# Bias lines of a four-layer attention kernel: 24 copies written from many partitions, and the later layers' lines made in the first layer

## The chip, the cores and the metric

One NeuronCore of a Trainium2 chip runs the whole program in one launch. The metric is device time in microseconds (us), the median of the runs. The engines are named as the profile names them: PE (TensorE, matrix products), PEld (its weight loads), DVE (VectorE), ACT (ScalarE), POOL (GpSimd) and SP, the engine that issues all DMAs of this kernel on one queue.

## The reference

The input is 512 tokens of 1,024 channels. Four layers follow one another, each `x + mixer(rms_norm(x) @ w_in) @ w_out`, in float32:

```
A  sliding-window attention (window 128, 16 heads of 64, 4 key heads),
   logits + head_bias(rel_table, query - key), a sink per head, SiLU gate
B  sparse attention in three branches over one shared key/value side:
   compressed keys (31 blocks of 32 tokens through a small MLP),
   selected blocks (all of at most 8), window (512, the whole sequence);
   each with head_bias(rel_table, distance)
C  twice: mLSTM (4 heads), gated linear attention (2 x 2 heads), and
   attention over the 128 best keys of a cheap index score,
   logits + rel_bias[t5_bucket(key - query)] (4 heads of 128)
```

`head_bias` is a table lookup: 32 buckets of distance (exact up to 16 or 8, logarithmic above) by heads. The bias of a pair of tokens depends on their distance alone, so the bias matrix of a head is constant along its diagonals.

## The kernel before

The tokens are 4 blocks of 128 on the partitions. `norm_x` normalizes x and transposes it into a high and a low half (`xhi`, `xlo`). Every projection is three products a step (`gemm_n_slices`, L262 to L264, and `gemm_t_slices`, L282 to L284). Weights come in pieces: `load` fills one of three buffers `wraw` by a DMA on SP (L228), `split` makes the halves `whi` (ACT, L235) and `wlo` (DVE L237, POOL L247) in one of five. Which weights follow which is written out as a plan; the loads of the next projection are spread over the present one. Attention runs as steps (queries, scores, values, done), and projections are woven between the steps by hand-written lists (`FILL_A`, `FILL_B`, `EVENTS`).

The order of the instructions on each engine's queue is not that of the program text: a scheduler at build time plays the program through with a cost model and puts each engine's instructions, the DMA issues on SP too, into the order in which they would become ready. On the chip each queue then runs strictly in that order. Tiles with a tag share a fixed number of buffers: the tag `E` has 4 (`epage`). It holds the exponentials of the attention, the split weights of the compression MLP, and the small pages of the bias code.

The bias code. `table33` puts a table of 32 buckets with a row of -1e30 below it into SBUF as [33, heads]. `toeplitz` multiplies it with a constant one-hot matrix [33, 384] (L369), which gives a line: the bias at distances 255 to -128 for each head. The result is copied out of PSUM (L371) and written to DRAM 128 times over (L373), from as many partitions as there are heads. `toeplitz_read` then reads a matrix [128 queries, heads, 256 keys] in which each query starts one element earlier than the one before it (L378); each query reads a copy of its own:

```
d = s.dram.tile([P, nh, 384], F32, name=name)
nc.sync.dma_start(d.rearrange("q h u -> h q u"), sb[:, None, :].to_broadcast([nh, P, 384]))
```

There are three lines. line_a (16 heads) is made in layer A behind the keys, line_b (16 heads) at the start of layer B, line_d (4 heads) in `consts_c` at the start of the first layer C. Each group of four heads of A and B reads its `bias` when its queries are projected; each of the two tasks of two heads in each layer C reads `dbias` (L1617). Layer B makes besides a bias `cb` for its compressed keys: four loads of one-hot pages (L816), 16 products (L817), one copy (L818).

Of the kernel before, what the change touches and what calls it, by code (L numbers as in the profile page):

```python
# [21 lines left out]
NT = 4  # L22
# [54 lines left out]
class Ctx:  # L77
# [25 lines left out]
    def banks(s, name, t, sc):  # L103
        """8 banks: products of the projections, transposes, scores, values"""
        s.PSB = {"g": 2, "t": t, "s": sc, "o": 1}
        s.ps = s.pool(name, 1, space=PSUM)
# [28 lines left out]
    def rstd(s, ss, n, width, tag, bufs=2):  # L135
        """1 / sqrt(ss / width + EPS): first guess from the exponent, Newton"""
# [15 lines left out]
    def bcast_row(s, pool, src, n, name, **kw):  # L152
        """[n] in DRAM -> [P, n]"""
        t = pool.tile([P, n], F32, name=name, **kw)
        s.nc.sync.dma_start(t, bass.AP(tensor=src.tensor, offset=src.offset, ap=[[0, P], [1, n]]))
        return t

# [1 line left out]
    RAW, HI = 3, 5  # L159

    def w(s, key):
        """the weights of this name; those that follow in the plan are loaded and split in the course of their use"""
# [16 lines left out]
    def prefetch(s, held, blocks):  # L179
        """queues the next loads of the plan: [(part of the present use behind it, what to emit)]; held: pieces in use, free one by one in the last block"""  # L180
# [20 lines left out]
    def progress(s, n):  # L201
        """n products of the present use are emitted"""
# [11 lines left out]
    def piece(s, out, segs, kt0, u, n, ku, width, gain=None):  # L214
        """segs: list of (dram 2d AP, column, width, column in tile). out: (hi, lo, width) per kt"""
# [37 lines left out]
    def gemm_n_slices(s, wts, width, evac, lhs=None, toks=range(NT), tag="g"):  # L253
        """out[tok, width] = x @ w, three passes; stops after every 12 products"""
# [20 lines left out]
    def gemm_t_slices(s, wts, cols, evac, tag="g"):  # L275
        """out[cols, tok] = (x @ w)^T for each range of 128 columns."""
# [15 lines left out]
    def x_rstd(s, t):  # L292
        """1 / rms of block t of x"""
# [19 lines left out]
    def norm_x(s, gain=None):  # L313
        """x / rms(x) * gain -> xhi, xlo; without a gain the weights bring it"""
# [21 lines left out]
    def load_gains(s):  # L336
        """the gains of the two norms of the second layer: those of 128 channels in a column"""
# [9 lines left out]
    def to_T(s, o, oT, ts):  # L347
        """o [P, 256] -> oT (hi, lo) [P, 2, ts]"""
# [14 lines left out]
    def toeplitz(s, table33, nh, line, name):  # L363
        """[33, nh] table and [33, 384] one-hot line -> DRAM [P, nh, 384], P times the same; [h, u]: the bias at distance 255 - u"""
        nc = s.nc
        ln = s.epage()[:33, :384]
        nc.sync.dma_start(ln, s.ia[line])
        ps = s.bk("t")
        nc.tensor.matmul(ps[:nh, :384], table33, ln, start=True, stop=True)  # L369
        sb = s.epage()[:nh, :384]  # L370
        nc.vector.tensor_copy(sb, ps[:nh, :384])  # L371
        d = s.dram.tile([P, nh, 384], F32, name=name)
        nc.sync.dma_start(d.rearrange("q h u -> h q u"), sb[:, None, :].to_broadcast([nh, P, 384]))  # L373
        return d

    def toeplitz_read(s, out, d, h0, nh):
        """out [P, nh, 256]: query p, key column k' of the blocks (previous, own): distance p + 128 - k'"""
        s.nc.sync.dma_start(out, bass.AP(tensor=d.tensor, offset=d.offset + h0 * 384 + 127,  # L378
                                         ap=[[d.shape[1] * 384 - 1, P], [384, nh], [1, 256]]))

    def table33(s, src, nh, name):
        t = s.cst.tile([33, nh], F32, name=name)
        s.nc.sync.dma_start(t[:32], src)
        s.nc.vector.memset(t[32:33], NEG)
        return t

# [1 line left out]
    def silu2(s, out, ps, th=None):  # L388
        """2 * silu(ps)"""
# [6 lines left out]
    def sumsq(s, out, src, sq, nh, hd, eng=None):  # L396
        """src [P, nh * hd] in SBUF -> out [P, nh] sums of squares"""
# [8 lines left out]
    def q_group(s, wts, wk, out):  # L406
        """projects 4 query heads and their gates; -> (raw queries [P, NT, 256], 1 / rms [P, NT * 4]), [2 * silu(gate)] per block"""
# [15 lines left out]
    def q_packs(s, q, t, wk):  # L423
        """queries of 4 heads, block t: normalized, -> [(hi 64, lo 64), head, tok] in F32R"""
# [13 lines left out]
    def q_packs2(s, q, t, wk):  # L438
        """queries of 4 heads, block t: normalized, -> for each pair of heads [(hi; hi) / (lo; lo), tok] in F32R"""
# [19 lines left out]
    def k_pack(s, kv, out, wk, bank="t", tag="qs"):  # L459
        """keys [P, heads, 64] -> out [(hi; lo), heads, tok] in F32R"""  # L460
# [10 lines left out]
    def half(s):  # L471
        """the next half of the bank o"""
# [10 lines left out]
    def pipeline_slices(s, steps):  # L483
        """attention steps, each in its stages behind those of its followers; yields the part of a step's work behind it"""
# [9 lines left out]
    def weave(s, main, fill):  # L494
        """main yields the part of the whole that is behind it; fill: [(number, products)], spread over it"""
# [14 lines left out]
    def pipeline(s, steps, fill):  # L510
        """attention steps, each in its stages behind those of its followers; fill: products [(first step, last step, number, slices)], one after the other"""
# [22 lines left out]
    def k_packs(s, kr, r, gain, kT, wk, t):  # L534
        """kr [P, 256] raw keys of 4 heads, r [P, 4]; kT[:, h, 0 / 1, tok]: (hi; hi) / (lo; lo)"""
# [16 lines left out]
    def out_plan(s, src, kt0):  # L552
        """the loads of 256 rows of src"""
        return [([(src, n * 512, 512, 0)], kt0, 2, 512) for n in range(2)]

    def w_out_slices(s, ws, lhs):
        """x += y[:, rows] @ the weights of these rows"""
# [20 lines left out]
# projections spread over the steps of the attention: from, to  # L578
# [3 lines left out]
def layer_a(s):  # L582
    nc, tc, ia = s.nc, s.tc, s.ia
    outer = s.stack
    with ExitStack() as st:
# [6 lines left out]
        # per-head constants  # L592
# [8 lines left out]
        # keys and values  # L601
# [19 lines left out]
        def project(g):  # L621
            """queries and gates of four heads"""
# [8 lines left out]
        class Step:  # L631
            """block t of the queries of group g"""
# [68 lines left out]
        for _ in project(0):  # L701
            pass
        what = {"q": (96, project), "o": (48, out)}
# [9 lines left out]
def compress(s, wk, R, w1, w2, posT):  # L713
    """R 2 x [P (head, chunk), 8 * 64] -> 2 * silu(flat @ w1), transposed: [P hidden, 2, P rows], and w2 [P, 2, 64]"""
# [57 lines left out]
# projections spread over the steps of the attention: from, to  # L772
# [4 lines left out]
def layer_b(s):  # L777
    nc, tc, ia = s.nc, s.tc, s.ia
    outer = s.stack
    with ExitStack() as st:  # L780
# [8 lines left out]
        # gains  # L789
# [9 lines left out]
        cb = lp.tile([P, 16, 16], F32, name="cb")  # L799
        gt = lp.tile([P, NT, 48], F32, name="gt")  # L800

        line = s.toeplitz(s.rel33, 16, "c_line_b", "line_b")
        # position embeddings: [(l 2, d), kt] by a transpose
# [7 lines left out]
        # bias of the compressed keys: [query, head, chunk - 8 * block + 8]  # L811
        pt = s.bk("t")
        for c in range(16):
            if c % 4 == 0:
                oc = s.epage()[:33].rearrange("p (a b) -> p a b", a=4)
                nc.sync.dma_start(oc, ia["c_cmp"][:, c:c + 4])  # L816
            nc.tensor.matmul(pt[:, c * 16:(c + 1) * 16], oc[:, c % 4], s.rel33, start=True, stop=True)  # L817
        nc.vector.tensor_copy(cb, pt[:, :256].rearrange("p (c h) -> p h c", h=16))  # L818
        # compressed branch: raw keys and values bounce to (head, chunk) rows
# [8 lines left out]
        # selected and window branches  # L828
        def rescale(t):
            """the gain of the queries' norm comes on to block t"""  # L830
# [41 lines left out]
        # keys of the compressed branch  # L872
# [11 lines left out]
        # values of the compressed branch, block diagonal over the heads of a group  # L884
# [869 lines left out]
```

## Time and profile before

| what | value |
|---|---|
| median of 3 runs | 2139.19 us (2138.87 to 2147.04) |
| span of the profiled execution, first to last instruction | 2134.7 us (no own time is listed beside it) |
| busy: PE, PEld, DVE, ACT, POOL | 1995.8, 1647.8, 1402.0, 928.7, 920.5 us |
| DMA | 168.58 MB, 79 GB/s in the mean |

A row of a timeline gives the start, the time, the engine, the line of the kernel, the operation with what it writes and reads, the number of instructions that are merged into the row, and in brackets the idle time of the engine ahead of it with what ended that. SPq is SP's DMA queue. Products of the PE overlap, so the distance of their starts counts, not their duration.

### The profile page before, as it was taken

What the parts mean: (1) busy time and instruction counts of PE and PEld (TensorE: products, weight loads), DVE (VectorE), ACT (ScalarE), POOL (GpSimd) and SP (SyncE); (2) the same over time, 40 slices, a digit from 0 to 9 for tenths busy, and PEclk for the clock granted to TensorE, in tenths of its full rate; (3) what the DMA queues carried; (4) which work ended last, traced back from release to release, by engine and by line L of the source; (5) the groups of instructions that cost most, each with busy time, mean ns of one, the idle gap of its engine ahead of it and who ended that gap; (6) DMA issues with size and microseconds to landing.
All of it is one profiled execution on the core that took longest, in us unless ns stands there. A gap on an engine that the chain in (4) does not pass through costs nothing.

```text
span 2134.7 us, 30245 instructions
## 1 busy us (share of the span) xinstructions
PE 1995.8 (93%) x10211; PEld 1647.8 (77%) x10211; DVE 1402.0 (66%) x3717; ACT 928.7 (44%) x2153; POOL 920.5 (43%) x866
## 2 busy tenths in 40 slices
PE   7789969999999998599899999999999999999999
PEld 6678857788888887377778788887777778788887
DVE  6267736846555576279986965556579976965555
ACT  4355425555454554254442433434454432433433
POOL 3434413544544431133765453344234755453343
PEclk9989989999999999799999999999999999999999
DMA  5632265321221101322222223232222222223231
GB/s 171 94 98 67 75 90 143 114 79 50 71 64 47 60 8 45 79 77 69 67 82 87 80 76 95 68 102 76 80 79 66 77 76 83 80 76 101 62 103 44
DMA packets 161339, 168.58 MB, mean 79 GB/s; under 512 B 25797, under 2 KB 135964, under 8 KB 161184
## 3 DMA queue, kind: packets, MB, share of 16 engines
q1 hardware_dynamic: 161184, 166.65, 27.5%
q8 instruction: 81, 1.33, 0.3%
q14 instruction: 74, 0.61, 0.1%
HBM read 155.08 MB, written 11.53 MB: 78 GB/s over the span
## 4 chain that ended last, share of the span: by engine, by line
PE 55%; DVE 15%; issue 4%; DMA 3%; POOL 1%; ACT 1%; SPq 0%; DVEq 0%; POOLq 0%; ACTq 0%
PE b_g L262 10%; PE b_g L263 10%; PE b_g L264 10%; PE b_g L282 3%; PE b_g L283 3%; PE b_g L284 3%; PE b_o L1059 2%; DVE wlo L237 2%; DVE topw L1310 2%; DMA line_d<-E 2%; PE b_s L1029 2%; DVE m L1309 1%; PE b_t L1052 1%; PE b_o L1536 1%; DMA wraw<-in_w_in_dram 1%
## 5 line engine op out<-in xcount | busy, mean ns | idle before, releaser
L247 POOL TENSOR_TENSOR wlo<-wraw,whi 128x512 fp32r<-128x512 f32 (+1 forms) x314 | 462.7, 1493 | 370.4 <-ACT whi L235 338.0
L262 PE MATMUL b_g<-whi,xhi 128*128 128x512 f32 x1280 | 508.2, 398 | 10.8 <-DVE my L1493 5.6
L264 PE MATMUL b_g<-whi,xlo 128*128 128x512 f32 x1280 | 508.2, 397 | 2.0 <-DVE xlo L360 2.0
L263 PE MATMUL b_g<-wlo,xhi 128*128 128x512 f32 x1280 | 507.3, 397 | 0.0
L235 ACT ACTIVATE whi<-wraw 128x1024 fp32r<-128x1024 f32 (+2 forms) x250 | 260.8, 1045 | 194.1 <-PE b_g L264 87.1
L262 PEld LDWEIGHTS b_g<-whi,xhi 128*128 128x128 f32 x1280 | 242.7, 190 | 64.2 <-issue 6.0
L264 PEld LDWEIGHTS b_g<-whi,xlo 128*128 128x128 f32 x1280 | 242.8, 190 | 54.1 <-DVE xlo L360 3.4
L263 PEld LDWEIGHTS b_g<-wlo,xhi 128*128 128x128 f32 x1280 | 242.7, 190 | 47.8 <-POOL wlo L247 0.4
L237 DVE TENSOR_TENSOR wlo<-wraw,whi 128x512 fp32r<-128x512 f32 (+2 forms) x198 | 188.4, 955 | 104.2 <-ACT whi L235 101.3
L282 PE MATMUL b_g<-xhi,whi 128*128 128x512 f32 x400 | 162.7, 407 | 29.5 <-ACT whi L235 22.8
L562 DVE TENSOR_TENSOR x<-x,b_g 128x512 f32<-128x512 f32 x192 | 130.1, 680 | 55.2 <-PE b_g L264 53.9
L283 PE MATMUL b_g<-xlo,whi 128*128 128x512 f32 x400 | 159.9, 400 | 0.0
L284 PE MATMUL b_g<-xhi,wlo 128*128 128x512 f32 x400 | 159.6, 399 | 0.2 <-POOL wlo L247 0.2
L282 PEld LDWEIGHTS b_g<-xhi,whi 128*128 128x128 f32 x400 | 75.9, 190 | 51.5 <-ACT whi L235 24.0
L284 PEld LDWEIGHTS b_g<-xhi,wlo 128*128 128x128 f32 x400 | 75.8, 189 | 19.0 <-issue 1.5
L283 PEld LDWEIGHTS b_g<-xlo,whi 128*128 128x128 f32 x400 | 75.9, 190 | 17.8 <-issue 2.5
L1059 PEld LDWEIGHTS b_o<-v,PT 128*128 128x128 f32 x640 | 82.1, 192 | 8.1 <-DVE PT L1055 3.2
L1493 DVE SCALAR_TENSOR_TENSOR my<-b_g,vec,my 128x511 f32<-128x511 f32 (+2 forms) x96 | 71.5, 744 | 21.3 <-ACT my L1490 19.9
L1059 PE MATMUL b_o<-v,PT 128*128 128x64 f32 x640 | 82.3, 269 | 3.3 <-DVE PT L1055 2.8
L957 POOL TENSOR_TENSOR og<-og,sz 128x256 f32<-128x256 f32 x32 | 24.3, 760 | 140.5 <-DVE og L951 132.4
L1499 POOL TENSOR_TENSOR mT<-my,mT 128x512 fp32r<-128x512 f32 x32 | 45.8, 1438 | 86.8 <-ACT mT L1498 52.8
L1039 ACT ACTIVATE E<-E,nm 128x256 f32<-128x256 f32 (+1 forms) x128 | 60.8, 476 | 35.2 <-DVE nm L1038 35.2
(419 smaller groups left out, 4150.7 us busy)
## 6 DMA issues: line engine op xcount, KB each, us to landing
wraw<-in_w_in_dram SPq DMA_DIRECT2D x240, 256.0 KB, 3.1
wraw<-in_b_w_in_dram SPq DMA_DIRECT2D x64, 256.0 KB, 3.1
wraw<-in_w_out_dram SPq DMA_DIRECT2D x32, 512.0 KB, 3.6
wraw<-in_w_in_dram SPq DMA_DIRECT2D x24, 512.0 KB, 4.8
wraw<-in_a_w_in_dram SPq DMA_DIRECT2D x32, 256.0 KB, 2.8
wraw<-in_kv_w_dram SPq DMA_DIRECT2D x12, 512.0 KB, 3.9
wraw<-in_a_w_out_dram SPq DMA_DIRECT2D x8, 512.0 KB, 3.5
wraw<-in_b_w_out_dram SPq DMA_DIRECT2D x8, 512.0 KB, 3.8
```

Source lines behind the costliest of these rows:

```text
L235: nc.scalar.activation(hi[:, :n, c], raw[:, :n, c], AF.Copy)
L237: nc.vector.tensor_tensor(lo[:, :h, c], raw[:, :h, c], hi[:, :h, c].bitcast(F32), OP.subtract)
L247: nc.gpsimd.tensor_tensor(lo[:, js, c], raw[:, js, c], hi[:, js, c].bitcast(F32), OP.subtract)
L262: nc.tensor.matmul(ps[:, :width], xh, h[:, :width], start=k == 0, stop=False)
L263: nc.tensor.matmul(ps[:, :width], xh, l[:, :width], start=False, stop=False)
L264: nc.tensor.matmul(ps[:, :width], xl, h[:, :width], start=False, stop=k == n - 1)
L282: nc.tensor.matmul(ps, h[:, c * P:(c + 1) * P], s.xhi[:, k], start=k == 0, stop=False)
L283: nc.tensor.matmul(ps, h[:, c * P:(c + 1) * P], s.xlo[:, k], start=False, stop=False)
L284: nc.tensor.matmul(ps, l[:, c * P:(c + 1) * P], s.xhi[:, k], start=False, stop=k == n - 1)
L562: nc.vector.tensor_tensor(s.x[:, t, n * 512:(n + 1) * 512], s.x[:, t, n * 512:(n + 1) * 512], ps, OP.add)
L1059: nc.tensor.matmul(bl.po[:, h * 64:(h + 1) * 64], PT[:, k * P:(k + 1) * P], v[b][:, k, g * 64:(g + 1) * 64], start=k == 0, stop=k == t)
L1493: nc.vector.scalar_tensor_tensor(y[:, j:], ps[:, :SEQ - j], w, y[:, j:], op0=OP.mult, op1=OP.add)
```

## The change

A line is written in 24 copies instead of 128. For that the table is repeated along its columns (8 times for 16 heads, 24 times for 4), so that one product gives a line for each copy and head on a partition of its own; three products, copies and writes make the 24 copies of a line of 16 heads, one of each those of a line of 4 heads. Query p = 16 a + b of a read uses copy a + b. A read is split into one DMA for each head. The lines of B and C and the bias `cb` are made in layer A, right behind the projection of its first four query heads; `cb` and the wider tables lie in the pool of constants. Comments and docstrings go too.

```
+    COPIES = 24
     def toeplitz(s, table33, nh, line, name):
         nc = s.nc
         ln = s.epage()[:33, :384]
         nc.sync.dma_start(ln, s.ia[line])
-        ps = s.bk("t")
-        nc.tensor.matmul(ps[:nh, :384], table33, ln, start=True, stop=True)
-        sb = s.epage()[:nh, :384]
-        nc.vector.tensor_copy(sb, ps[:nh, :384])
-        d = s.dram.tile([P, nh, 384], F32, name=name)
-        nc.sync.dma_start(d.rearrange("q h u -> h q u"), sb[:, None, :].to_broadcast([nh, P, 384]))
+        d = s.dram.tile([s.COPIES, nh, 384], F32, name=name)
+        n = min(s.COPIES, P // nh)
+        for c in range(0, s.COPIES, n):
+            ps = s.bk("t")
+            nc.tensor.matmul(ps[:n * nh, :384], table33[:, :n * nh], ln, start=True, stop=True)
+            sb = s.epage()[:n * nh, :384]
+            nc.vector.tensor_copy(sb, ps[:n * nh, :384])
+            nc.sync.dma_start(d[c:c + n].rearrange("q h u -> (q h) u"), sb)
         return d
     def toeplitz_read(s, out, d, h0, nh):
-        s.nc.sync.dma_start(out, bass.AP(tensor=d.tensor, offset=d.offset + h0 * 384 + 127,
-                                         ap=[[d.shape[1] * 384 - 1, P], [384, nh], [1, 256]]))
+        w = d.shape[1] * 384
+        for h in range(nh):
+            s.nc.sync.dma_start(out[:, h], bass.AP(tensor=d.tensor, offset=d.offset + (h0 + h) * 384 + 127,
+                                                   ap=[[w - 16, 8], [w - 1, 16], [1, 256]]))
     def table33(s, src, nh, name):
-        t = s.cst.tile([33, nh], F32, name=name)
-        s.nc.sync.dma_start(t[:32], src)
-        s.nc.vector.memset(t[32:33], NEG)
+        nc, n = s.nc, min(s.COPIES, P // nh)
+        t = s.cst.tile([33, n * nh], F32, name=name)
+        nc.sync.dma_start(t[:32, :nh], src)
+        nc.vector.memset(t[32:33], NEG)
+        nc.vector.tensor_copy(t[:32, nh:].rearrange("p (n h) -> p n h", h=nh), t[:32, None, :nh].to_broadcast([32, n - 1, nh]))
         return t
+    def later_biases(s):
+        nc = s.nc
+        s.line_b = s.toeplitz(s.rel33, 16, "c_line_b", "line_b")
+        s.line_d = s.toeplitz(s.table33(s.ia["rel_bias_2"], 4, "rel33d"), 4, "c_line_d", "line_d")
+        s.cb = s.cst.tile([P, 16, 16], F32, name="cb")
+        pt = s.bk("t")
+        for c in range(0, 16, 4):
+            oc = s.epage()[:33].rearrange("p (a b) -> p a b", a=4)
+            nc.sync.dma_start(oc, s.ia["c_cmp"][:, c:c + 4])
+            for j in range(4):
+                nc.tensor.matmul(pt[:, (c + j) * 16:(c + j + 1) * 16], oc[:, j], s.rel33[:, :16], start=True, stop=True)
+        nc.vector.tensor_copy(s.cb, pt[:, :256].rearrange("p (c h) -> p h c", h=16))
...
# layer_a
         for _ in project(0):
             pass
+        s.later_biases()
...
# layer_b
-        cb = lp.tile([P, 16, 16], F32, name="cb")
+        cb, line = s.cb, s.line_b
-        line = s.toeplitz(s.rel33, 16, "c_line_b", "line_b")
-        pt = s.bk("t")
-        for c in range(16):
-            if c % 4 == 0:
-                oc = s.epage()[:33].rearrange("p (a b) -> p a b", a=4)
-                nc.sync.dma_start(oc, ia["c_cmp"][:, c:c + 4])
-            nc.tensor.matmul(pt[:, c * 16:(c + 1) * 16], oc[:, c % 4], s.rel33, start=True, stop=True)
-        nc.vector.tensor_copy(cb, pt[:, :256].rearrange("p (c h) -> p h c", h=16))
...
# consts_c
-    t = s.table33(ia["rel_bias_2"], 4, "rel33d")
-    s.line_d = s.toeplitz(t, 4, "c_line_d", "line_d")
```

## Rows read from the trace of the kernel before

**Rows 1.** The page: the span, and PE busy in tenths of 40 slices.

```profile
span 2134.7 us, 30245 instructions
PE   7789969999999998599899999999999999999999
```

**Rows 2.** Busy time by stretch: PE, PEld, DVE, ACT, POOL, granted clock, DMA share, GB/s.

```profile
94.70:114.80 20.10, 0.03 (x2) 0.06 (x1) 0.68 (x7) 0.00 (x0) 1.70 (x2) 0.58 0.81 125
114.80:120.00 5.20, 5.20 (x21) 4.55 (x22) 3.26 (x19) 3.30 (x13) 2.04 (x3) 0.65 0.94 308
303.90:322.90 19.00, 0.43 (x2) 0.01 (x1) 0.00 (x0) 0.13 (x1) 0.00 (x0) 0.65 0.88 111
322.90:332.00 9.10, 9.05 (x33) 7.91 (x34) 3.98 (x6) 3.17 (x8) 2.38 (x2) 0.60 0.88 273
867.20:890.10 22.90, 0.16 (x1) 0.00 (x0) 0.00 (x1) 1.06 (x1) 0.00 (x0) 0.55 0.26 42
...
120.00:260.00 140.00, 139.99 (x886) 123.80 (x885) 104.46 (x341) 69.91 (x219) 63.13 (x66) 1.00 0.22 70
980.00:1100.00 120.00, 108.93 (x515) 87.72 (x513) 118.05 (x264) 53.25 (x94) 76.57 (x74) 1.00 0.27 82
```

**Rows 3.** Timeline of SP and DVE in layer A.

```profile
76.43 0.35 SPq L373 DMA_DIRECT2D line_a<-E  x1
110.22 0.92 SPq L378 DMA_DIRECT2D bias<-line_a  x2
...
75.86 0.53 DVE L371 COPY E<-b_t 16x384 f32<-16x384 f32 x1
...
114.12 0.29 DVE L660 CUSTOM_DVE_ANT_0 E<-b_s,bias 128x128 f32<-128x128 f32 x1 [26.90 <-DMA bias<-line_a]
```

**Rows 4.** Timeline of PE in layer A.

```profile
88.45 0.67 PE L657 MATMUL b_s<-kT,qT 128*128 128x128 f32 x5
...
94.09 0.39 PE L264 MATMUL b_g<-whi,xlo 128*128 128x512 f32 x1
94.32 0.39 PE L262 MATMUL b_g<-whi,xhi 128*128 128x512 f32 x1
114.78 2.05 PE L657 MATMUL b_s<-kT,qT 128*128 128x256 f32 x8 [20.07 <-DVE mx L660]
```

**Rows 5.** Timelines of SP and PE in layer B.

```profile
288.11 0.33 SPq L373 DMA_DIRECT2D line_b<-E  x1
...
293.76 1.95 PE L817 MATMUL b_t<-rel,E 33*128 33x16 f32 x16
...
322.95 3.60 PE L817 MATMUL b_t<-rel,E 33*128 33x16 f32 x16 [18.62 <-DMA E<-in_c_cmp_dram]
```

**Rows 6.** Timelines of SP, PE, ACT and POOL in layer C.

```profile
854.04 0.27 SPq L373 DMA_DIRECT2D line_d<-E  x1
...
887.62 0.39 SPq L378 DMA_DIRECT2D dbias<-line_d  x1
...
890.12 0.80 PE L282 MATMUL b_g<-xhi,whi 128*128 128x512 f32 x1 [22.76 <-ACT whi L235]
...
897.67 0.50 PE L282 MATMUL b_g<-xhi,whi 128*128 128x512 f32 x1 [2.17 <-DVE ik L360]
...
889.01 1.06 ACT L235 ACTIVATE whi<-wraw 128x1024 fp32r<-128x1024 f32 x1 [29.29 <-DMA wraw<-in_w_in_dram]
...
857.49 3.50 POOL L247 TENSOR_TENSOR wlo<-wraw,whi 128x512 fp32r<-128x512 f32 x2 [0.81 <-ACT whi L235]
```

**Rows 7.** A stretch of line_a's write; DMA issues: KB each, us to landing.

```profile
76.40:88.00 11.60, 11.60 (x54) 9.28 (x53) 1.84 (x5) 4.42 (x10) 2.71 (x4) 1.00 0.79 90
...
kvd<-kvc SPq DMA_DIRECT2D x4, 256.0 KB, 2.2
dbias<-line_d SPq DMA_DIRECT2D x4, 256.0 KB, 3.5
```

**Rows 8.** Timeline of PE: the line product of layer A.

```profile
74.95 0.82 PE L369 MATMUL b_t<-E,rel 33*16 33x384 f32 x2
```

## The prediction

> **What bounds the kernel now.** I read the page first. TensorE (PE) is busy nearly everywhere; only a few of the forty slices (of 53.4 us) stand at 5 to 8 tenths after the start, and slices 2, 3, 6, 17 lie where bias lines are written [rows 1]. Then I cut those places into stretches at the ends of the PE's waits [rows 2]: in 94.7 to 114.8, 303.9 to 322.9 and 867.2 to 890.1 us all five engines together do almost nothing (PE 0.03, 0.43 and 0.16 us). These are no shifts of load between engines; everything stops. The reader should see in the same rows that the clock granted to the PE is 0.55 to 0.65 there, that is, it has gone to the lower level (1.2 GHz) after an idle PE, and is still low in the two stretches that follow here; and that from 120 to 260 the PE has no gap at all, so what is lost in a stop is not won back behind it.
>
> The timelines name each stop. In the first layer (A) one write of line_a goes out at 76.43, the reads of bias and the weight loads behind them leave SP only at 110.22, and VectorE (DVE) waits 26.90 us for the bias [rows 3]. The PE's next instruction, scores, waits 20.07 us [rows 4]. In the second (B) line_b goes out at 288.11, later one-hot loads of the compressed-key bias stand behind it on the same queue, and the PE's product on the last of them waits 18.62 us [rows 5]. In the third (C) line_d goes out at 854.04, the read of dbias waits for it until 887.62, weight loads stand behind that read, ACT waits 29.29 us for one, and the PE 22.76 us for its split [rows 6].
>
> Why are these writes slow? Line_a is 3 MB from 16 partitions, so 2,048 rows of 1.5 KB; line_d is 0.75 MB from 4, so 512 rows; both take 33.6 to 33.8 us [rows 3, 6]. The DMA engines are busy to 0.81 in the first stop and to 0.26 in the last [rows 2], which fits 16 engines and 4 engines with 128 rows each: 33.6 / 128 = 0.26 us a row on one engine.
>
> **The change part by part.**
>
> *The writes.* A line now has 24 copies. For 16 heads that is three writes of 128 partitions with one row each, for 4 heads one write of 96 partitions. At 0.26 us a row and 8 rows an engine a write takes 2.1 us of engine time; the nearest whole write, 256 KB of kvd from 128 partitions, lands after 2.2 us [rows 7]. So a line is in DRAM 2.2 us (below) to 3 x 2.1 + 2.2 = 8.5 us (above) after its last copy; I take 5. The engines are free from about 77 us, and the first scores can be used from 89 us (the PE runs their products at 88 [rows 4]): line_a written by 83, read by 87. The stop in A is gone. In B and C no write is left; B loses its one-hot loads too, and C's read of dbias has nothing to wait for.
>
> *Gain of A.* 20.07 us [rows 4], and what the low clock costs behind it: 5.2 us of work at a granted 0.65 [rows 2] would take 3.4 at the full clock, 1.8 less. Together 21.9 us.
>
> *Gain of B.* 18.62 us. Behind it 9.1 us of work run at a granted 0.60 [rows 2], 3.6 lost; 1.65 of that shows in 16 small products, 3.60 us there against 1.95 ahead of the stop [rows 5]. One line product, 0.82 us [rows 8], and the 32 small ones, 3.9 us at the full clock, leave this layer. 26.9 us.
>
> *Gain of C.* 22.76 us. The 12 products behind it end, with a further wait of 2.17, at 897.67, 7.55 us after 890.12 [rows 6]; at the full clock a product starts 0.23 after the other [rows 4], which makes 2.8, so 4.8 more can go. The 2.17 I take for a consequence: ScalarE (ACT) evacuates the narrow projection only behind the late weights in its queue, and DVE behind ACT. Plus 0.82 for the line product: 28.4 us. Will weights be late next? The page for the fourth piece of the index weights comes free when GpSimd (POOL) ends at about 861 [rows 6]; 3.5 us for a load of that size [rows 7], 1.1 for the ACT and 1.8 for the POOL split [rows 6] make it ready near 867.4, and the PE wants it near 868.6. The margin is 1 us.
>
> *Cost in A.* The PE gets two more products for line_a, three for line_b and one for line_d, 6 x 0.82 = 4.9, and the 32 small ones, 3.9: 8.8 us, on a PE that has no gap, so in full. The copies on DVE (0.53 each [rows 3], seven) fall into 76 to 88, where DVE is busy 1.84 of 11.6 us [rows 7]: nothing; without that cover 3.7.
>
> *Pages.* The later lines take 10 pages of the tag E, line_a 4, and the tag has 4 buffers; the first two attention steps stand behind them and need 2 each. A page lives for a load (2.2 to 3.5 us by kvd and dbias [rows 7]) and its product, or for a copy and its write: 3 to 4.8 us. 14 / 4 rounds make 10 to 17 us from 75, so pages are free for scores at 86 to 92 instead of 89. The PE has projections until 94.3 [rows 4], and 8.8 us of the new products besides. So nothing, or a few us if these in-order products wait for their loads one after the other: 0 to 15, I take 2.
>
> *Reads.* Each read becomes one a head: 4 for 1, eight times, and 2 for 1, four times: 28 more issues of 0.39 us on SP [rows 6]. Queued behind them are weight loads with three buffers in hand; 1.2 us a group costs nothing while the PE has split weights left, and 1.2 x 8 = 9 if not. I take nothing for the point. Two reads of 512 KB (1,024 rows) are through 3.9 us after their issue [rows 3], so a row of 1 KB costs one of 16 engines at most 0.06 us. Line_d's write, with 4 heads outermost, kept about 4 engines busy [rows 2]; the new reads lie as 8 x 16 rows, so they may run on 8: a group's reads are then 64 rows an engine instead of 32, 2 us more (above) or nothing (below). Only A's first group could show it; I take nothing.
> The Trainium skill (DMA: Bandwidth & Descriptors, Rules for kernel authors) speaks against this edit: the slowest dimension of the access patterns sets how many engines a DMA gets, so an outermost size of 8 confines it to 8. The shares of line_a and line_d agree; of an 8 x 16 read no run here shows it yet. By the rule the sum would be up to 2 us worse, 2079; I stay with the bound below, as the PE has other products then.
>
> *Start.* The table is now copied along its columns on DVE, which waits for its load, behind x and the first weights. The order could put it ahead of the norm: 0 to 3 us, I take 1. The plan of all queues is worked out anew from the changed program, so other places move: I take 3.5 us against, between 10 won and 10 lost: where DVE is full, 980 to 1100 us, the PE stands idle for 11.1 us [rows 2], and another order can give or take about as much as that.
>
> *Sum.* 21.9 + 26.9 + 28.4 - 8.8 = 68.4; less 2 + 1 + 3.5 = 62. The profiled span is 2134.7; no own time of this execution is listed beside it, and the median of the runs lies 4.5 above. 2134.7 - 62 = 2072.7 of span, plus 4.5: 2077 us.
>
> **The rivals.**
> 1. *A new stop in A.* PE products of the later lines wait, in order, for E pages and loads, with the scores behind them. For it: six loads in a chain of four buffers. Against: the PE has other products, and SP and the engines are nearly idle there. Five loads at 2 to 3 us exposed beyond what I took are 10 to 15 us: 2087 to 2092.
> 2. *The lines stay slow, so the change doesn't do what it says.* If a write costs by its landing in DRAM and not by rows per engine, A keeps its stop. Against: kvd's 2.2 us. B and C still win 55, A pays 8.8 and the 6.5 of new waits: 2139 - 40 = 2099.
> 3. *The reads become slow (slower than before).* Sixteen partitions now read overlapping parts of one copy. If a read row then costs what a written row does, 0.26 us, and if 8 engines share it as 4 did line_d, a group's 64 rows take 16.8 us, 13 more than the 3.9 seen. Eight groups make 103 us, 2077 + 103 = 2180 if nothing hides them. It decides from 62 / 8, about 8 us exposed a group. For it: no trace shows shared copies. Against: from 120 to 260 us, where A's groups 1 to 3 use theirs, the PE has no gap [rows 2], so those reads have time in hand.
>
> **How the numbers follow.** Forecast 0.79, with its own range from 2139.2 - 68.4 - 10 = 2061 to 2139.2 - 68.4 + 2 + 3 + 10 = 2086; rival 1 0.14; rival 2 0.03; rival 3 0.03; 0.01 for no change. The range, 2061 to 2098, takes in the first two with some 6 us of those losses on top of rival 1, and leaves out the others. Half a percent (10.7 us) is about what a measurement here can tell from no change: faster 0.96, same 0.01, slower 0.03.
>
> **What would show it.** Right: no stretch of all idle engines near 95, 304 or 867; the granted clock at 1 there; writes of lines that land in under 5 us; line and bias products near 80 to 100 in A and none in B or C. Wrong in A: the PE waits at a line or bias product, or at scores, for a load or a page. Wrong in C: ACT waits for weights before the index product. Wrong in the reads: DVE's first scores of a group wait for bias. The forecast fails if a stop that I take for the writes' is another's: a load that is as late without them.

## The result, and the profile after

The changed kernel takes 2077.34 us in the median (2075.24 to 2081.21, 4 runs), the kernel before in the same session 2141.44 (2138.87 to 2147.04, 4 runs): a ratio of 0.9702, 95% interval 0.9681 to 0.9724. The forecast was 2077.0. The profiled execution has a span of 2074.1 us, 60.6 less than before.

The page of the changed kernel, which answers to [rows 1]: the slices at 5 to 7 tenths behind the start are gone; three stand at 8.

```profile
PE   7999999999999998999999999998999899999999
```

Where the 60.6 us came from is read best from a balance of the PE: its idle time and its busy time by region, with the borders at about the same places of the work (the last scores of A, the first part of B, the last values of B, a point in the first C). In A's stretch the PE has 13 more instructions in the changed kernel, where the change adds 44: some 30 products from A's end fall into the next stretch there. No idle time lies at that border, so only busy time is shifted by it. Columns: the stretch, its length, busy time of PE, PEld, DVE, ACT, POOL with instruction counts, granted clock, DMA share, GB/s. Busy time by stretch of the kernel before:

```profile
60.00:240.00 180.00, 159.92 (x964) 139.23 (x963) 108.10 (x361) 81.15 (x236) 79.18 (x81) 0.94 0.38 87
240.00:360.00 120.00, 98.05 (x467) 79.45 (x465) 61.27 (x142) 41.84 (x98) 36.48 (x30) 0.90 0.54 115
360.00:824.00 464.00, 447.18 (x2712) 386.57 (x2710) 287.27 (x1082) 248.65 (x741) 204.76 (x220) 0.99 0.20 60
824.00:1032.00 208.00, 173.93 (x765) 132.05 (x766) 136.99 (x308) 87.91 (x162) 64.50 (x53) 0.93 0.25 69
1032.00:2130.00 1098.00, 1068.12 (x5098) 872.40 (x5097) 770.38 (x1732) 441.41 (x862) 515.09 (x466) 1.00 0.26 79
```

The same view of the changed kernel:

```profile
60.00:224.00 164.00, 164.00 (x977) 140.60 (x976) 105.86 (x360) 81.91 (x237) 75.65 (x78) 0.99 0.26 82
224.00:328.00 104.00, 95.40 (x474) 78.37 (x473) 67.36 (x155) 44.01 (x106) 38.71 (x33) 0.97 0.41 111
328.00:790.00 462.00, 446.07 (x2708) 386.66 (x2705) 286.89 (x1075) 246.73 (x732) 207.05 (x220) 0.99 0.21 59
790.00:970.00 180.00, 171.43 (x761) 132.53 (x761) 134.55 (x303) 87.75 (x162) 62.99 (x51) 0.98 0.26 74
970.00:2070.00 1100.00, 1070.38 (x5099) 873.92 (x5099) 770.96 (x1736) 441.19 (x862) 514.86 (x467) 0.99 0.27 79
```

Length less busy time is the idle time. It fell from 20.1 to 0 in A, from 22.0 to 8.6 around the start of B, from 34.1 to 8.6 around the start of C, and stayed within 1 us in the other two: 60.1 us in all. The busy time by the page is 1995.8 us before and 1995.4 after. So nearly all of the gain is idle time, and the busy time, which by the prediction's terms should have fallen by some 5 us net, did not. The experiments below ask what made the idle time go, and why the busy time stayed.

SP's queue in the timeline of the changed kernel, which answers to the SP rows of [rows 3, 5, 6]:

```profile
77.68 6.32 SPq L377 DMA_DIRECT2D line_a<-E  x2
84.53 0.32 SPq L377 DMA_DIRECT2D line_a<-E  x1
86.53 5.66 SPq L384 DMA_DIRECT2D bias<-line_a  x8
92.29 1.36 SPq L377 DMA_DIRECT2D line_b<-E  x3
100.10 0.32 SPq L377 DMA_DIRECT2D line_d<-E  x1
...
789.64 1.22 SPq L384 DMA_DIRECT2D dbias<-line_d  x2
```

The last write of line_a is issued at 84.53, and the read that waits for it at 86.53: if the read leaves as soon as the write is through, a write lands within 2.0 us, where the one write before took 33.8 us [rows 3]. The time of line_a is now that of its products, which stand among projections on the PE (at 76.2 and 82.1), not of the DMA. line_b and line_d follow by 101, and C's read of dbias is an issue among others. Two more stretches of the changed kernel, columns as above: the last two line_a writes, and the reads behind them.

```profile
84.00:87.00 3.00, 3.00 (x14) 2.46 (x14) 0.35 (x2) 0.00 (x0) 0.00 (x0) 1.00 0.41 148
89.00:92.00 3.00, 3.00 (x12) 1.69 (x10) 1.38 (x4) 1.06 (x1) 1.62 (x3) 1.00 0.52 168
```

In the first, 0.41 of 16 engines over 3 us is 19.7 engine-us for two writes (256 rows) and a one-hot load: at most 0.08 us a row, where the old line had 0.26. In the second, 0.52 of 16 engines is the work of 8 engines; no other transfer is issued between 86.53 and 92.19, so 25 engine-us for some 490 rows of 1 KB make 0.05 us a row.

The PE's timeline of the changed kernel in A, where its products for the lines and the compressed-key bias now stand; this answers to [rows 4, 5]. In the traces each product of a line or of `cb` appears as two instructions: the 16 products of `cb` are the "32 small products" of this text.

```profile
102.14 1.06 PE L407 MATMUL b_t<-rel,E 33*128 33x16 f32 x8
103.14 0.66 PE L457 MATMUL b_t<-ident,qs 128*128 128x128 f32 x4
103.72 1.96 PE L407 MATMUL b_t<-rel,E 33*128 33x16 f32 x16
105.61 1.11 PE L680 MATMUL b_s<-kT,qT 128*128 128x128 f32 x8
106.64 1.06 PE L407 MATMUL b_t<-rel,E 33*128 33x16 f32 x8
107.64 0.76 PE L457 MATMUL b_t<-ident,qs 128*128 128x128 f32 x4
...
109.05 0.63 PE L264 MATMUL b_g<-whi,xlo 128*128 128x512 f32 x1
109.48 0.63 PE L262 MATMUL b_g<-whi,xhi 128*128 128x512 f32 x1
...
112.24 0.39 PE L264 MATMUL b_g<-whi,xlo 128*128 128x512 f32 x1
112.47 0.39 PE L262 MATMUL b_g<-whi,xhi 128*128 128x512 f32 x1
```

There is no idle time in brackets, and from 60 to 224 us the PE is busy throughout (first stretch above): no line product, no small product and no first scores wait. But the products behind 108 start 0.43 us apart, those behind 112 start 0.23 apart: the granted clock stands at the lower level for some 3.5 us, though the PE has not paused. Before, the same 0.43 was seen behind the stops, and the prediction took it for their consequence.

### The profile page after: what moved, and what is told of

It reads as the page before. It is cut to its first block, busy times and chain, and to the rows that moved or that the text cites. A ratio compares the mean times of both kernels' runs of the same rounds, so it can differ in the third digit from the quotient of the medians.

```text
span 2074.1 us, 30341 instructions
## 1 busy us (share of the span) xinstructions
PE 1995.4 (96%) x10219; PEld 1650.1 (80%) x10219; DVE 1404.1 (68%) x3723; ACT 928.6 (45%) x2153; POOL 919.6 (44%) x866
## 4 chain that ended last, share of the span: by engine, by line
PE 60%; DVE 15%; issue 4%; DMA 2%; POOL 1%; ACT 1%; SPq 0%; DVEq 0%; POOLq 0%; ACTq 0%
PE b_g L262 11%; PE b_g L263 11%; PE b_g L264 11%; PE b_g L282 4%; PE b_g L283 4%; PE b_g L284 4%; PE b_o L1074 3%; DVE wlo L237 2%; PE b_s L1044 2%; DVE topw L1325 1%; PE b_o L1551 1%; PE b_t L1067 1%; DVE m L1324 1%; DMA wraw<-in_w_in_dram 1%; DVE x L585 1%
## 5 line engine op out<-in xcount | busy, mean ns | idle before, releaser
L1074 PEld LDWEIGHTS b_o<-v,PT 128*128 128x128 f32 x640 | 82.1, 192 | 7.3 <-DVE PT L1070 3.2
L1047 DVE CUSTOM_DVE_ANT_0 E<-b_s,bias 128x256 f32<-128x256 f32 (+1 forms) x128 | 49.0, 385 | 41.5 <-PE b_s L1044 24.6
```

What stands on the lines that cost most here:

```text
L1074: nc.tensor.matmul(bl.po[:, h * 64:(h + 1) * 64], PT[:, k * P:(k + 1) * P], v[b][:, k, g * 64:(g + 1) * 64], start=k == 0, stop=k == t)
```

## The experiments

Ratios, with their 95% intervals, are against the kernel before in the same session (its medians: 2137.5 to 2141.4 us).

**1. Which half of the change brings it?** `copies_only` has the new writes and reads with every line and `cb` in its old place; `move_only` has the old 128-copy write and single read with all lines and `cb` made in A.

```
# copies_only: later_biases() is left out; in layer_b and consts_c as before
         line = s.toeplitz(s.rel33, 16, "c_line_b", "line_b")
# move_only: toeplitz, toeplitz_read, table33 as before, and
+        s.later_biases()
```

> The new writes and reads, but line_b, the compressed-key bias and line_d made where the kernel before makes them. Theory (each stop comes from a write that takes 33 us, and 24 copies from many partitions take under 8): the stops of B and C go as well, so within 8 us of the changed kernel's 2077: layer A is 7 us shorter on the PE, B pays three line products and the 32 small ones (6), C one product and 0 to 4 us while SP waits for the write of line_d. Rival (moving the work away is what frees B and C): two stops stay, 19 and 23 us with their low clock, so about 2120.

> 128 copies from few partitions and one read a group as in the kernel before, but line_b, line_d and the compressed-key bias made in layer A. Theory (the writes are slow wherever they stand): three writes of 33 us follow one another on one queue in A with weight loads behind them, so A's stop of 20 us becomes 40 to 80 us; B and C give back 47 to 55; 2115 to 2165. Rival (work in A hides the writes, the move alone brings most): A's stop stays at 20 and the PE pays 6 us there, so about 2095.

copies_only: 2076.71 us (2074.67 to 2078.84), ratio 0.9706 [0.9691, 0.972]. move_only: 2150.09 (2145.9 to 2153.76), ratio 1.0046 [1.003, 1.0062]. The cheaper write, with the reads that belong to it, is the whole gain as far as these runs can tell; the move alone makes the kernel 0.5% slower. Both came as the theory had it. A stretch of move_only in A, columns as above:

```profile
120.00:130.00 10.00, 0.15 (x1) 0.00 (x0) 0.00 (x0) 0.00 (x0) 0.00 (x0) 0.67 0.87 97
```

The longest wait of ACT in move_only from 76 to 170 us (in total, times, longest):

```profile
ACT whi L235 <- DMA wraw<-in_a_w_in_dram: 57.1, 1, 57.1
```

Two slow writes, issued at 77.6 and 88.4, follow one another on the DMA engines, which are busy to 0.87 while the PE has nothing; bias is read at 111.8 only, and ACT waits 57.1 us for weights behind them. The stops were brought together, not removed.

**2. Is it the number of copies or where they come from?** `copies128` is the changed kernel with 128 copies, each still from a partition of its own.

```
-    COPIES = 24
+    COPIES = 128
```

> The changed kernel with 128 copies instead of 24, so 16 writes of 128 partitions for a line of 16 heads and 4 for line_d. Theory of the prediction (0.26 us a row of 1.5 KB on one engine): 2,048 rows on 16 engines take 33 us for line_a and for line_b, 8 us for line_d, A's stop is back and 20 to 60 us long: 2100 to 2140. Rival (what costs is that a partition's one row is fetched 128 times): 16 writes of 196 KB at the pace of kvd (256 KB in 2.2 us with its landing) are through in 10 to 20 us a line, and the PE pays 26 more line products (21 us) that overlap with nothing: 2095 to 2110 by products, with each write landing within 3 us of its issue.

2120.91 us (2118.4 to 2125.75), ratio 0.9915 [0.9897, 0.9933]: 44 us slower than with 24 copies. But the DMA engines are not the reason. SP issues 15 of line_b's 16 writes from 113.8 to 131.5 us; a stretch among them, columns as above:

```profile
120.00:130.00 10.00, 10.00 (x17) 5.18 (x16) 4.46 (x8) 0.00 (x0) 0.00 (x0) 0.50 0.43 156
```

The PE's timeline in copies128, the products of line_b:

```profile
112.28 19.59 PE L374 MATMUL b_t<-E,rel 33*128 33x384 f32 x32 [2.28 <-DMA E<-in_c_line_b_dram]
```

The same 3 MB leave from all partitions at 156 GB/s with 0.43 of the engines, where move_only's leave from 16 partitions at 97 GB/s with 0.87. Per byte that is a share of 0.0028 against 0.0090, 3.2 times cheaper. So the slow part of the old write was not the amount and not its landing in DRAM; it was the source, the rows of few partitions, each fetched 128 times over. (Whether the few partitions or the repetition makes it slow was not separated.) What the 24 copies save over 128 are products: 29 more line products stand on the PE here. Those of line_b run one behind the other at the lower clock, 0.61 us an instruction where the changed kernel takes 0.37 (six in 2.20 us at 90.12). The busy time by the page is 2039.4 us against 1995.4. So the time lies in the theory's range, but the way there is the rival's: no long stop in A, and products that overlap with nothing. The rival's 2095 to 2110 was too low, as it took the products at the full clock.

**3. Each stop by itself.** Three kernels are the kernel before with the new write and read for one line alone, left in its place.

```
-        line = s.toeplitz(s.rel33, 16, "c_line_a", "line_a")
+        line = s.toeplitz_n(s.widen(s.rel33, 16, "rel33w"), 16, "c_line_a", "line_a")
...
-            s.toeplitz_read(bias, line, 4 * g, 4)
+            s.toeplitz_read_n(bias, line, 4 * g, 4)
```

> Only the first layer's line goes out in 24 copies and is read a head at a time; the lines of layers B and C keep their 128 copies and their places. If each stop stands by itself and is the write's, this wins A's term: 20.07 us of wait and 1.8 of low clock, less two more line products (1.6), so 20 us, 2119; the writes of line_a are through by 87 us and the stops of B (18.6 us) and C (22.8 us) stay as they were. If, as the rival has it, time won in A is partly given back behind it (a later load or page is no earlier), it wins under 15 us: above 2124.

> Only the second layer's line goes out in 24 copies, still made in B, with the one-hot loads of the compressed-key bias behind it on the queue. By the theory 18.6 us of wait and 3.6 of low clock go and two more line products come (1.6): 20.6 us, 2118.5. By the rival the start of B stops for something else (in the kernel that moves the lines too, the place ahead of B lost some 7 us that the kernel before did not lose): 10 to 14 us, 2125 to 2129.

> Only the third layer's line goes out in 24 copies (one write of 96 rows), still made at the start of C. By the theory 22.8 us of wait and 4.8 of low clock go: 27.5 us, 2111.5, with the read of dbias leaving its queue within 4 us of the write. If the time is saved in each stop by itself, the gains of this kernel and of the two that change A's or B's line alone add up to the 62.5 us of the kernel with all three (2076.7) within 6 us. By the rival the weights behind dbias are late on their own: half of it stays, 2123 or more.

| kernel | median us | won | ratio | expected gain |
|---|---|---|---|---|
| line_a alone | 2122.61 (2120.59 to 2127.9) | 14.9 | 0.993 [0.9911, 0.9949] | 20 |
| line_b alone | 2125.31 (2124.26 to 2127.97) | 12.2 | 0.9943 [0.9925, 0.996] | 20.6 |
| line_d alone | 2108.0 (2106.71 to 2113.38) | 29.5 | 0.9863 [0.9845, 0.9881] | 27.5 |

The three gains add up to 56.6, 5.9 short of copies_only's 62.5 and so just within the 6 us that were set as the bound; C came 2 us above the expected gain, A at the rival's bound, B at the rival's middle. The rival's reason is not what the trace shows, though. Busy time by stretch of the line_b kernel, beside the row of the kernel before (240 to 360):

```profile
240.00:342.00 102.00, 98.64 (x468) 78.98 (x466) 61.30 (x143) 41.49 (x96) 35.17 (x29) 0.95 0.38 109
```

The idle time of the start of B fell from 22.0 to 3.4: 18.6, exactly the stop. What came back is mostly busy time, 2002.6 us by the page against 1995.8, of which the two added line products explain 1.6. In the same kernel, the PE's timeline in B:

```profile
300.74 4.43 PE L847 MATMUL b_t<-rel,E 33*128 33x16 f32 x32
...
306.97 0.63 PE L264 MATMUL b_g<-whi,xlo 128*128 128x512 f32 x1
307.39 0.63 PE L262 MATMUL b_g<-whi,xhi 128*128 128x512 f32 x1
```

The stop is gone, yet 12 products behind the 32 small ones still start 0.43 us apart. At 0.2 us more each that is 2.4 of the 3.6 us that the prediction credited to the end of the stop. (In the kernel before, 16 of the 32 stand ahead of the stop, at 293.76, and the products behind those are not slow; here all 32 stand together.) The line_a kernel too wins its stop and loses busy time. Its idle time in A fell by the whole 20.1, the stops in B (18.8) and in C (22.7) stayed, and its busy time by the page is 2001.9 against 1995.8. Busy time by stretch of the line_a kernel:

```profile
60.00:222.00 162.00, 162.00 (x981) 141.16 (x980) 110.91 (x367) 82.67 (x238) 79.03 (x81) 1.00 0.27 83
...
808.00:1020.00 212.00, 177.75 (x762) 134.96 (x763) 135.14 (x305) 87.46 (x161) 64.12 (x52) 0.90 0.24 67
```

Around C, where nothing of it was changed, it is busy 3.8 us longer for the same products, at a granted clock of 0.90 against 0.93: its PE waits 2.8 us for `oT` there, which the kernel before does not, and the lower clock follows (0.64 from 810 to 820 us). We put that to the order of the queues, which was worked out anew; no run tests it. Busy time by stretch of the line_d kernel at the same place:

```profile
824.00:1010.00 186.00, 176.40 (x777) 135.77 (x778) 141.67 (x320) 88.90 (x163) 70.19 (x61) 0.97 0.27 80
```

Its idle time fell from 34.1 to 9.6, and here the low clock behind the stop went with it: the busy time by the page is 1991.0, 4.8 less than before, where 2.6 was credited.

**4. Are the small products what lowers the clock, and what is their place worth?** `cb_in_b` is the changed kernel with `cb` made in B as before; `wide` has the small products 128 columns wide.

```
# cb_in_b: the loop over c_cmp is moved from later_biases back to layer_b
# wide
-                nc.tensor.matmul(pt[:, (c + j) * 16:(c + j + 1) * 16], oc[:, j], s.rel33[:, :16], ...)
+                nc.tensor.matmul(pt[:, j * P:(j + 1) * P], oc[:, j], s.rel33, ...)
```

> The changed kernel, but the compressed-key bias (four one-hot loads, 32 small products, one copy) stays in layer B. Theory: the 3.9 us of small products move from A to B, each where the PE is full, so no change within 5 us of 2077; in A the clock stays at its upper level at 108 to 111 us, where it fell behind these products. Rival (its loads in E pages hold up the first scores in A): 5 to 10 us faster.

> The changed kernel with the 32 small products of the compressed-key bias made 128 columns wide (the whole widened table) in place of 16; four copies take the 16 columns that count. In three kernels the granted clock falls to 0.5 behind these 32 products, though the PE has no gap there. Theory: it is these products and not a stop that brings the lower level; with 128 columns they last as long (about 0.13 us each, as 128-column transposes do, 4.1 us in all), the granted clock stays at 1.00 through 100 to 115 us, and the time falls by what the low clock cost, 1 to 2 us: 2075.5. Rival: the dip has another cause (the change from one kind of product to another, or the interleaving with scores): the dip stays, 2077. A third possibility: 128 columns cost more than 0.13 us each, 2080 or more.

cb_in_b: 2071.8 us (2069.63 to 2075.53), ratio 0.9684 [0.9669, 0.97], just outside the theory's 5 us and at the near edge of the rival's range; part 7 comes back to it. wide: 2077.74 (2071.17 to 2080.97), ratio 0.9698 [0.9677, 0.9719]. In cb_in_b the dip went with the products: from 100 to 110 us the granted clock is 1.00, though the PE pauses there for 1.5 us, and in B the products behind the small ones start 0.43 apart, with no pause ahead. Its PE's timeline in B:

```profile
274.97 3.95 PE L831 MATMUL b_t<-rel,E 33*128 33x16 f32 x32
278.85 0.79 PE L262 MATMUL b_g<-whi,xhi 128*128 128x512 f32 x1
279.44 0.63 PE L263 MATMUL b_g<-wlo,xhi 128*128 128x512 f32 x1
```

In wide the 32 products lasted the same (3.83 us), but the dip did not go, as the rival had it. It was longer, with a granted clock of 0.50 from 108 to 114 us, behind a pause of 0.68 us. wide's PE in the timeline:

```profile
101.99 3.83 PE L407 MATMUL b_t<-rel,E 33*128 33x128 f32 x32
...
107.09 1.77 PE L680 MATMUL b_s<-kT,qT 128*128 128x128 f32 x8 [0.68 <-ACT qT L458]
```

So the clock falls behind these 32 products in three orders of the work without any pause of the PE (the changed kernel, the line_b kernel, cb_in_b), and needs no stop. That the 16 columns are to blame is not shown: with 128 the theory's 1.00 did not come, but a pause stands there too. Which property of the products does it stays open.

**5. Do the reads on eight engines cost anything?** `reads16` turns the two sizes of a read around: query p = 8 a + b reads copy a + b.

```
-                                                   ap=[[w - 16, 8], [w - 1, 16], [1, 256]]))
+                                                   ap=[[w - 8, 16], [w - 1, 8], [1, 256]]))
```

> The changed kernel, with query p = 8 a + b reading copy a + b, so that a read's outermost size is 16 and not 8, the same bytes and the same rows. If the outermost size sets how many engines a read gets, its packets fall on 16 engines instead of 8 and a bias read lands sooner; the theory is that nothing waits for these reads, so the time is that of the changed kernel, 2077 within 4 us. By the rival (a group's reads up to 2 us late, twelve groups) it would be 5 to 24 us faster: 2053 to 2072.

2075.15 us (2073.63 to 2076.7), ratio 0.9704 [0.969, 0.9719], the changed kernel's own. The stretch of the same reads in reads16, columns as above:

```profile
88.00:91.00 3.00, 3.00 (x12) 1.66 (x10) 1.38 (x4) 1.06 (x1) 1.62 (x3) 1.00 0.81 162
```

The share rises from 0.52 to 0.81, so more than 8 engines work; the rate stays (162 against 168 GB/s), and fits the pace at which SP issues reads of 128 KB, one every 0.7 to 0.8 us (8 in 5.66 us in the changed kernel); what sets that pace was not tested. The rule of the Trainium skill (DMA: Bandwidth & Descriptors, Rules for kernel authors), that the slowest dimension sets how many engines a transfer gets, is borne out by the 0.52. Its price here is nothing: the one wait that the two traces put down to a bias read, 4.1 us of POOL for `dbias`, is in the kernel before as well.

**6. A better place for the products?** `early` makes all lines and `cb` ahead of the first norm, where the PE is idle for its first 9 us, with the table's load ahead of x; `early_wide` has the wide products besides.

```
+        line = s.toeplitz(s.rel33, 16, "c_line_a", "line_a")
+        s.later_biases()
         s.norm_x(ia["a_norm"][0])
```

> As the run beside it, with the 16-column products as the change has them. Theory: 1 to 2 us above the wide one if the low clock behind the small products falls on work of the PE, the same if the PE waits there anyway for x; else as the other: 2071.

> All lines and the compressed-key bias are made ahead of the first norm, the table loaded ahead of x, with the wide products of the run beside it. Theory: in the first 9 us the PE waits for x and is idle, so up to 8.8 us of products that cost their full time in the changed kernel are hidden; against that x and the first weights come later by the bytes put ahead of them and behind (0.4 MB of loads and 1.3 MB of writes at about 400 GB/s, up to 4 us). 2070, between 2066 and 2076. Rival: the DMA engines are full from 4 us on, so the products wait for one-hot lines in order and hold up the transposes of x behind them: 2080 to 2090.

Both lose 27 us to the changed kernel and lie outside every range that was given: 2104.32 (2103.47 to 2104.78), ratio 0.9829 [0.9813, 0.9846], and 2104.45 (2102.44 to 2104.67), 0.9828 [0.9811, 0.9845]. The waits of the PE in the first 60 us of early (in total, times, longest):

```profile
PE b_t L374 <- DVE rr L149: 16.8, 1, 16.8
PE b_t L374 <- DMA E<-in_c_line_b_dram: 9.5, 1, 9.5
PE b_t L374 <- issue: 7.8, 1, 7.8
PE b_t L407 <- DMA E<-in_c_cmp_dram: 2.0, 1, 2.0
```

The first product comes at 16.8, where it comes at 9.0 in the changed kernel. Then the seven loads (three lines, four one-hot pages) go through four `E` pages, a page comes free only behind the product, or the copy and the write, that uses it, and the PE stands in its order at them: a chain from 16.8 to past 46 us with 19.3 us of waits, and no other product between. In all the PE is idle for 36.0 of the first 60 us, against 11.9. This is the mechanism of the rival, and of the prediction's first rival, at a place without cover; its 2080 to 2090 was too low. In A the same chain runs from 76 to 107 us under projections and costs no wait.

**7. The best parts together.** `cb_in_b_16` is cb_in_b with the reads of reads16.

> The fastest kernel so far (the compressed-key bias made in B again, 2071.8) with the 16 x 8 reads. Theory: the reads change nothing and the place of the 32 small products is worth 3 to 5 us, since in B they stand where the PE has no gap either but A's first scores no longer wait behind them: 2070 to 2074, a ratio to the kernel before of 0.966 to 0.969. Rival: the 5 us between that kernel and the changed one are the accident of one order of the queues, which any edit redraws: 2075 to 2079.

2073.25 us (2072.49 to 2075.66), ratio 0.9694 [0.9678, 0.971]. The time is within the theory's range and the ratio just above it, and its interval overlaps that of the changed kernel. Both kernels with `cb` in B have medians 4 to 5.5 us below the changed kernel's, but neither interval stands clear of its own, so a version that beats it is not shown, and neither is what the place of the small products is worth.

## Why the prediction was right, and where its sizes were off

The forecast was a gain of 62 us; the medians of one session differ by 64.1, the two profiled executions by 60.6.

**The stops were the writes'.** This step held as put: A's 20.07, B's 18.62 and C's 22.76 with the 2.17 behind it are gone, and C's next weights were not late, with a margin called 1 us. copies_only and the three single kernels show that the new write, with its reads, does it.

**Gain of A, cost in A.** Idle time fell by 20.1 as forecast. The pages cost 0 where 2 was taken: no wait in brackets. The start cost 0 where 1 was taken: the PE is idle for 11.9 of the first 60 us in both kernels. The copies on DVE and the reads cost nothing, as said; the first scores stand behind the PE's own products and wait for no bias. The 8.8 us of products are real (4.6 for the lines beyond line_a's first product, 4.1 for the small ones by their rows), but that the move itself gains nothing was hidden in the sum: 5.5 us of these products are only taken from B and C, and 3.3 are new. Taken from there and put here, the move cancels, and copies_only and the changed kernel agree with that (ratios 0.9706 and 0.9702).

**Gain of B.** Idle time around its start fell by 13.4, not 18.6. The rest came back as waits at the join of A and B. The waits of the PE in the changed kernel from 224 to 328 us (in total, times, longest):

```profile
PE b_g L264 <- DVE xlo L360: 3.2, 1, 3.2
PE b_s L752 <- DMA R<-kvd: 1.9, 1, 1.9
PE b_g L262 <- DVE x L585: 1.2, 1, 1.2
PE b_g L262 <- DVE rr L142: 1.1, 1, 1.1
```

With smaller ones they make 8.6; beside its stop the kernel before waits 3.3 there (2.0 of it on `xlo`, too). DVE is nearly full at that place: it is busy 5.83 of 6 us from 254 to 260. This is the term "order", taken at 3.5 for the whole kernel; here alone it is 5.3, and 1.8 of it is won back elsewhere. In the line_b kernel (idle 22.0 to 3.4) it is absent, so it belongs to this order of the work and not to the write.

**The clock terms were mis-sized.** 1.8, 3.6 and up to 2.6 us (C's 4.8 without its wait) were credited to the end of the low clock, 8 in all. With the products that the change adds on balance (8.8 - 5.5 = 3.3), busy time should have fallen by 8.0 - 3.3 = 4.7 us; by the two pages it fell by 0.4. A page is one execution, and the runs of the kernel before alone go from 2135.4 to 2147.0 us, so this difference by itself shows little; the rows show more. In A some 8 products behind the small ones are 0.2 us late each, 1.6 us, about what the end of A's stop was to give. In B the line_b kernel has 2.4 of the 3.6 back behind its 32 small products (part 3), and in the changed kernel the longer wait at the join has a lower clock behind it (0.58 from 260 to 266 us). C's term held (the line_d kernel). What made the sum right is that the waits taken at 6.5 (pages, start, order) came to about 3.5: 63.6 of idle time against the 60.1 that fell. Two errors of 3 to 4 us, one each way, nearly cancel. That the median came within 1 us of the forecast is luck; that the gain is the three stops is not.

**The price of a write row.** 0.26 us a row on an engine, read from the old line, was carried over to the new writes. It is at most 0.08 there, and the last write was through in 2.0 us where 5 was taken for a line. Yet line_a, expected to be written by 83, was through at 86.5, since its products stand apart on the PE. Neither mattered, since A's first scores come at 105.6, behind the PE's products.

**The rivals.** The lines did not stay slow (part 2), the reads are not slow (0.05 us a row where the rival feared 0.26), and no stop arose in A (part 6 shows the conditions in which it would).

## What to carry to other kernels

A stop in which all engines stand still gave back its whole length as idle time when its cause was mended in its place (20.1, 18.6 and 24.5 us here). The time won need not be the same (14.9, 12.2 and 29.5): the low clock behind a stop is won only if nothing else there lowers it, so look at what stands between the stop and the slow products, and take single gains of a few us with care where an edit draws the order of all queues anew. A write that fetched the same few partitions over and over was worth turning into one from many partitions, with the repetition made by a product; moving it to another place only moved the stop. In-order products that wait for small loads through few buffers cost no wait here under other work of the PE, and 19 us of waits where there was none.

## What was not expected of the hardware

The granted clock of the PE fell to the lower level behind 32 products of 33 rows by 16 columns (0.13 us apart) with no idle time ahead: 12 products 0.43 us apart in place of 0.23 in the line_b kernel, about 8 in the changed one. In copies128 it stood at 0.50 for 10 us in which the PE, without a gap, ran line products of 33 rows. And the same 3 MB left SBUF at a DMA share of 0.43 and 156 GB/s from 128 partitions, but at 0.87 and 97 GB/s from 16.
